# A small HBM-to-HBM copy ahead of the sine load on ScalarE's DMA queue in a rotary embedding kernel

## The chip, the cores and the metric

The kernel runs on one core of a Trainium2 chip. The metric is device time in microseconds (us): the median of the runs shown. Beside the runs there is one profiled execution, whose span goes from its first to its last instruction. The engines of the core are TensorE (PE, with its weight load PEld), VectorE (DVE), ScalarE (ACT), GpSimd (POOL) and SyncE (SP). DMAs are issued from SP (queue q1 in the profile) and from ScalarE (queue q10), and 16 DMA engines carry out both queues' transfers.

## The reference

The input x has the shape 8 x 2048 x 8 x 64 (batch, position, head, feature; float32, 33.55 MB), cos and sin have 2048 x 32 (256 KB each). The 64 features of a head are two halves, and each position turns them by its own angles:

```python
x1, x2 = x[..., :32], x[..., 32:]
out1 = x1 * cos - x2 * sin
out2 = x1 * sin + x2 * cos
return np.concatenate([out1, out2], axis=-1)
```

The output has the shape of x. All of x is read from HBM once and all of the output is written once.

## The kernel before

Positions go to the 128 partitions, 16 of them to each (lines 35 to 38). A batch is so one tile `xt` of 128 x 8192 float32 (4 MB), in which a partition holds 32 KB that lie together in HBM. There are five such buffers (line 45) for eight batches, and the result is written back into the tile in place.

Loads are issued from SP (`load`, lines 64 to 70). Batch 0 comes in three pieces (1, 1 and 2 MB), with the cosine table between the first and the second; the other batches come whole. The sine table is issued on ScalarE's queue, as the first DMA there (line 76). The first five batches are loaded at the start; the load of batch b + 5 is issued when batch b has been stored (lines 192 and 193), because it takes its buffer.

Stores are issued from ScalarE for batches 0 to 6 and from SP for batch 7 (`store`, lines 72 to 74). Batch 0 is stored in two halves, batch 7 in a half and two quarters, the others whole (`shares`, lines 177 to 182).

The work goes piece by piece (`pieces`, lines 170 to 175), mostly 2048 of a batch's 8192 elements per partition. For a piece, GpSimd makes the two products with the sine (line 122; `nsin` is the negated sine), VectorE the product with the cosine (line 129), and then

- kind A: VectorE adds them into `xt` (line 136);
- kind B: TensorE adds them by matmuls with a unit matrix (lines 143 and 144) and ScalarE copies the sum into `xt` (line 145);
- kind C: VectorE makes the product with the sine as well (line 148), TensorE adds, ScalarE copies (lines 160 to 165).

The first piece of batches 1 to 5 is of kind B or C (line 99), all else is of kind A. `keep` holds the instructions of each engine in the order in which they are written. Waits are put in by the framework: each DMA adds to one of a few completion counters, which are given out in turn, and an engine that needs the data, or a later DMA that takes the same counter, waits for it. Between the start and the first piece, ScalarE negates the sine and copies it to PSUM (lines 90 and 91), and VectorE copies the cosine to PSUM (line 93). GpSimd's first product waits for the sine and for the first piece of batch 0.

Of the kernel before, what the change touches and what calls it, by code (L numbers as in the profile page):

```python
# [10 lines left out]
def kernel(  # L11
# [7 lines left out]
    nc = tc.nc  # L19
    keep = tc.keep_in_program_order  # L20
# [51 lines left out]
    def store(b, lo, n):  # L72
        queue = nc.sync if b == last else nc.scalar
        keep(queue.dma_start(out=ov[b, :, lo : lo + n], in_=xts[b][:, lo : lo + n]))  # L74

    keep(nc.scalar.dma_start(out=sin_sb, in_=sin_src))
    for b in range(NBUF):
        load(b)
# [3 lines left out]
        out=eye,  # L82
        in_=eye,
# [140 lines left out]
```

## Time and profile before

| what | before |
|---|---|
| runs, median (lowest to highest) | 163.81 us (163.75 to 164.03), 3 runs |
| profiled execution, its span | 161.8 us (its time outside the span is not recorded) |
| VectorE busy | 140.1 us (87%) |
| GpSimd busy | 138.9 us (86%) |
| TensorE busy | 49.4 us (31%) |
| ScalarE busy | 12.8 us (8%) |
| DMA queues' packet time, share of 16 engines' span | q1 55.5%, q10 42.6% |
| moved by DMA | 67.65 MB, mean 418 GB/s |
| HBM read, written | 34.08 MB, 33.55 MB |
| sine: issued, landed | 0.73 us, 6.46 us |
| first store: issued, landed | 18.36 us, 38.06 us |
| last load landed | 134.32 us |
| last store: issued, landed | 156.0 us, 160.91 us |

The span of the profiled execution is the time from its first to its last instruction; the runs' times also hold what lies around it. Busy shares of engines are averages over the whole span. "Landed" is when the last of the 16 completion counts of a DMA arrived. A DMA packet is what one DMA engine moves in one piece; its record has a start, a duration, a size and a queue, but not the engine.

### The profile page before, as it was taken

The page shows a single profiled execution, that of the slowest core. Times are in us where ns is not written, and L with a number is a line of the kernel's source. Part 1 is how long each engine was busy: PE and PEld are TensorE (multiplying, and loading weights), DVE is VectorE, ACT ScalarE, POOL GpSimd, SP SyncE. Part 2 cuts the span into 40 slices and gives each one's busy share as a digit, 9 for nine tenths or more (in the row PEclk, how much of TensorE's full clock was granted, in tenths as well). Part 3 has the DMA queues.
Part 4 walks back from the last instruction along what each step waited for, and adds up shares of the span by engine and source line. Part 5 has one row for each costly group of instructions (what it writes and reads, how often), then busy time and mean ns, then how long its engine had stood idle before and what let it go on. Part 6 is the DMA issues. An engine that isn't in the chain of part 4 may idle for free.

```text
span 161.8 us, 459 instructions
## 1 busy us (share of the span) xinstructions
PE 49.4 (31%) x80; PEld 18.5 (11%) x80; DVE 140.1 (87%) x66; ACT 12.8 (8%) x14; POOL 138.9 (86%) x70
## 2 busy tenths in 40 slices
PE   0000000597309760978049714972000000000000
PEld 0000000142004220322023301330000000000000
DVE  0297999999999999999999999199989999899950
ACT  3300000002200220021000220022000000000000
POOL 1399997998999999992999959999899997999800
PEclk9999999999975998589957995699655555555555
DMA  5999999999999999899899999999999999999995
GB/s 158 425 454 494 413 308 446 413 470 405 462 405 462 389 502 405 389 510 397 389 510 397 389 512 397 397 502 397 397 488 413 405 478 413 405 478 409 397 419 225
DMA packets 3314, 67.65 MB, mean 418 GB/s; under 512 B 368, under 2 KB 368, under 8 KB 624
## 3 DMA queue, kind: packets, MB, share of 16 engines
q1 hardware_dynamic: 2016, 38.01, 55.5%
q10 hardware_dynamic: 1296, 29.62, 42.6%
q14 instruction: 2, 0.02, 0.0%
HBM read 34.08 MB, written 33.55 MB: 418 GB/s over the span
## 4 chain that ended last, share of the span: by engine, by line
DMA 48%; DVE 37%; POOL 9%; issue 2%; DVEq 0%; SPq 0%; POOLq 0%; ACTq 0%
DMA xt<-in_x_dram 26%; DVE t L129 18%; DMA out_dram<-xt 18%; DVE xt L136 17%; POOL t L122 9%; DMA sin_sb<-in_sin_dram 4%; DVE t L148 1%; DVEq L136 0%; SPq L67 0%; POOLq L122 0%; ACTq L74 0%
## 5 line engine op out<-in xcount | busy, mean ns | idle before, releaser
L122 POOL TENSOR_TENSOR t<-xt,sin_sb 128x1024 f32<-128x1024 f32 (+1 forms) x32 | 70.4, 2199 | 13.5 <-DMA xt<-in_x_dram 8.3
L129 DVE TENSOR_TENSOR t<-xt,cos_ps 128x2048 f32<-128x2048 f32 (+1 forms) x34 | 73.4, 2167 | 0.8
L122 POOL TENSOR_TENSOR t<-xt,nsin 128x1024 f32<-128x1024 f32 (+1 forms) x32 | 70.3, 2196 | 0.0
L136 DVE TENSOR_TENSOR xt<-t,t 128x2048 f32<-128x2048 f32 (+1 forms) x29 | 62.2, 2145 | 8.2 <-POOL t L122 5.5
L143 PE MATMUL o<-t,eye 128*128 128x512 f32 x24 | 17.0, 799 | 23.1 <-DVE t L129 19.6
L160 PE MATMUL o<-t,eye 128*128 128x512 f32 x16 | 12.0, 844 | 37.8 <-DVE t L129 35.6
L144 PE MATMUL o<-t,eye 128*128 128x512 f32 x24 | 14.9, 709 | 0.0
L145 ACT COPY xt<-o 128x1024 f32<-128x1024 f32 x6 | 6.1, 1012 | 45.7 <-PE o L144 45.7
L143 PEld LDWEIGHTS o<-t,eye 128*128 128x128 f32 x24 | 5.5, 256 | 32.5 <-issue 26.5
L160 PEld LDWEIGHTS o<-t,eye 128*128 128x128 f32 x16 | 3.7, 256 | 43.2 <-issue 39.4
L165 ACT COPY xt<-o 128x1024 f32<-128x1024 f32 x4 | 4.0, 1012 | 47.8 <-PE o L161 47.8
L93 DVE COPY cos_ps<-cos_sb 128x512 f32<-128x512 f32 x1 | 0.7, 695 | 6.9 <-DMA cos_sb<-in_cos_dram 6.9
L144 PEld LDWEIGHTS o<-t,eye 128*128 128x128 f32 x24 | 5.6, 234 | 8.2 <-issue 7.6
L161 PE MATMUL o<-t,neye 128*128 128x512 f32 x8 | 6.3, 875 | 0.2
L148 DVE TENSOR_TENSOR t<-xt,sin_ps 128x2048 f32<-128x2048 f32 x2 | 4.6, 2281 | 0.0
L161 PE MATMUL o<-t,eye 128*128 128x512 f32 x8 | 4.1, 592 | 0.0
L161 PEld LDWEIGHTS o<-t,neye 128*128 128x128 f32 x8 | 2.2, 300 | 5.3 <-issue 3.6
L161 PEld LDWEIGHTS o<-t,eye 128*128 128x128 f32 x8 | 1.5, 190 | 1.9 <-issue 1.9
L90 ACT ACT_TABLE_LOAD x1 | 1.3, 1283 | 1.2 <-PEq L208 1.2
L90 ACT ACTIVATE nsin<-sin_sb 128x512 f32<-128x512 f32 x1 | 0.6, 629 | 4.0 <-DMA sin_sb<-in_sin_dram 4.0
L91 ACT COPY sin_ps<-sin_sb 128x512 f32<-128x512 f32 x1 | 0.6, 580 | 0.0
L80 POOL MEMSET eye<- 128x128 f32 x1 | 0.2, 204 | 0.3 <-POOLq L208 0.3
(6 smaller groups left out, 1.0 us busy)
## 6 DMA issues: line engine op xcount, KB each, us to landing
xt<-in_x_dram SPq DMA_DIRECT2D x7, 4096.0 KB, 42.8
out_dram<-xt ACTq DMA_DIRECT2D x6, 4096.0 KB, 27.2
out_dram<-xt ACTq DMA_DIRECT2D x2, 2048.0 KB, 22.3
xt<-in_x_dram SPq DMA_DIRECT2D x2, 1024.0 KB, 6.7
xt<-in_x_dram SPq DMA_DIRECT2D x1, 2048.0 KB, 12.2
out_dram<-xt SPq DMA_DIRECT2D x1, 2048.0 KB, 9.9
out_dram<-xt SPq DMA_DIRECT2D x2, 1024.0 KB, 6.2
sin_sb<-in_sin_dram ACTq DMA_DIRECT2D x1, 256.0 KB, 5.7
```

The costliest lines, as they stand in the source:

```text
L90: keep(nc.scalar.mul(nsin, sin_sb, -1.0))
L93: keep(nc.vector.tensor_copy(cos_ps, cos_sb))
L122: nc.gpsimd.tensor_mul(out=t2u[:, :, u, :].rearrange("p (r h) d -> p r h d", h=H), in0=xu[:, :, 1 - u, :].rearrange("p (r h) d -> p r h d" ...
L129: nc.vector.tensor_mul(out=t1.rearrange("p (r k d) -> p r k d", r=nr, d=Dh), in0=xk, in1=rep(cos_ps[:, r0 : r0 + nr, :], 2 * H),)
L136: keep(nc.vector.tensor_add(out=xt, in0=t1, in1=t2))
L143: nc.tensor.matmul(oc, eye, t1[:, cs], start=True, stop=False)
L144: nc.tensor.matmul(oc, eye, t2[:, cs], start=False, stop=True)
L145: keep(nc.scalar.copy(xt[:, 2 * j * C : 2 * (j + 1) * C], o))
L148: nc.vector.tensor_mul(out=t2.rearrange("p (r k d) -> p r k d", r=nr, d=Dh), in0=xk, in1=rep(sin_ps[:, r0 : r0 + nr, :], 2 * H),)
L160: nc.tensor.matmul(oc, eye, t1u[:, gs, u, :], start=True, stop=False)
L161: nc.tensor.matmul(oc, eye if u else neye, t2u[:, gs, 1 - u, :], start=False, stop=True)
L165: nc.scalar.copy(xu[:, :, u, :], o.rearrange("p (g d) -> p g d", d=Dh))
```

## The change

A copy is issued on ScalarE's queue ahead of the sine. It takes 16 pieces of 512 bytes of batch 0 from x and puts them into the output at the same places. The pieces are the first 512 bytes of each sixteenth of the batch, 256 KB apart. Nothing passes through SBUF. What it writes is x itself, not the rotated values; the stores of batch 0 write the same bytes later, and wait for the copy.

```diff
         queue = nc.sync if b == last else nc.scalar
         keep(queue.dma_start(out=ov[b, :, lo : lo + n], in_=xts[b][:, lo : lo + n]))
 
+    W = 128
+    first = out.rearrange("b (q r) h d -> b q (r h d)", q=16)[0, :, :W]
+    keep(nc.scalar.dma_start(out=first, in_=x.rearrange("b (q r) h d -> b q (r h d)", q=16)[0, :, :W]))
     keep(nc.scalar.dma_start(out=sin_sb, in_=sin_src))
     for b in range(NBUF):
         load(b)
```

The order of the instructions on every engine is otherwise the same. The lines after it move down by three.

## The prediction

> **What bounds the kernel now.** I read the page's slices first, then its DMA queues, then the stretches by time, then the trace's single DMA packets, and the chain of waits last.
>
> The slices of the page give the mean busy share of the 16 DMA engines (tenths) and what they moved, in 40 slices of 4.05 us; below them stands the queues' share of the 16 engines' span (q1 is SP's queue, q10 ScalarE's).
>
> ```profile
> DMA  5999999999999999899899999999999999999995
> GB/s 158 425 454 494 413 308 446 413 470 405 462 405 462 389 502 405 389 510 397 389 510 397 389 512 397 397 502 397 397 488 413 405 478 413 405 478 409 397 419 225
> ...
> q1 hardware_dynamic: 2016, 38.01, 55.5%
> q10 hardware_dynamic: 1296, 29.62, 42.6%
> ```
>
> The two queues fill 98.1% of the engines' span, and only the first and the last slice are not full. The bound is the DMA engines, not VectorE (87%) or GpSimd (86%). The stretches say the same; columns: us, busy us (and count) of PE, PEld, DVE, ACT, POOL, then clock, DMA share and GB/s.
>
> ```profile
> 20.00:22.00 2.00, 0.00 (x0) 0.00 (x0) 1.90 (x2) 0.00 (x0) 2.00 (x2) 1.00 0.79 262
> 22.00:24.00 2.00, 0.00 (x0) 0.00 (x0) 1.97 (x2) 0.00 (x0) 2.00 (x2) 1.00 1.02 344
> ...
> 30.00:60.00 30.00, 20.05 (x32) 7.47 (x32) 29.35 (x13) 3.66 (x4) 29.26 (x14) 0.89 1.00 431
> 60.00:90.00 30.00, 15.85 (x24) 5.86 (x24) 29.38 (x14) 3.42 (x4) 27.00 (x13) 0.77 1.01 437
> 90.00:120.00 30.00, 13.46 (x24) 5.20 (x24) 25.41 (x13) 3.04 (x3) 27.50 (x13) 0.80 1.00 433
> ```
>
> From 30 us on the engines move 431 to 437 GB/s with no gap. There is one dip, slice 5 of the page (counted from 0; 308 GB/s, 20.2 to 24.3 us). Short stretches are rough, because a packet counts where it starts, so I sized the dip by the trace's packets. A load packet of 32 KB takes 1.213 us everywhere else; of those that start from 19.4 to 23.3 us, all 16 engines have some at 1.25 to 2.09 us. What they take beyond 1.213, summed and divided by 16, is 0.39 us per engine for those that start before 22 us and 0.45 us for those after: **0.83 us of every engine lost**, once. Before that there are 0.49 us in the first packets (0.35 to 1.03 us for 8 KB, against 0.309 later) and 0.15 us near 3 us; from 24 us to the end all of it comes to 0.06 us. The dip is where the first store of the run comes in: issued on ScalarE's queue at 18.36 us, its first packet recorded at 22.2 us. All later stores add no such loss, though each batch writes 4 MB of the output not touched before.
>
> The chain of waits names DMA and VectorE by turns:
>
> ```profile
> 62.55 28.82 DMA out_dram<-xt
> ...
> 91.50 42.82 DMA xt<-in_x_dram
> ...
> 134.45 4.62 POOL t L122 x2
> ```
>
> I don't read it as three equal limits. The store issued at 62.55 stands behind the store before it (issued 46.3, landed 72.0), and the load issued at 91.5 behind one that lands at 95.8: both queues always hold work, so an issue some tenths later costs the engines nothing. At the end the last three stores land at 156.05, 158.49 and 160.91 us, 2.43 apart, which is 8 packets of 8 KB at 0.309 (2.47): they too follow the engines' pace.
>
> So time = start of the first packet (1.76 us) + packet time per engine + losses + about 0.9 us after the last packets. An edit counts by what it adds to or takes from the engines.
>
> **The change, part by part.** The sum is made against the profiled span of 161.8 us. The profile gives nothing around it; the runs' median of 163.81 lies 2.0 above, and I leave that as it is.
>
> *One more issue on ScalarE's queue.* The sine's issue row is 0.40 us, the stores' 0.34: sine issue 0.73 -> about 1.1, table load 1.16 -> 1.55. The table load (1.28) ends at 2.8, under ScalarE's wait to 6.48: 0.
>
> *The sine's landing.* At the start each engine takes an 8 KB load packet (0.309) and a 2 KB sine packet (0.084) in turn. With the copy's packet ahead and an issue 0.4 us later, the sine falls one to three turns back, and then has cosine packets (0.084) in its gaps: it lands 0.04 to 0.30 us later than 6.46, I take 0.15. GpSimd waits for it:
>
> ```profile
> POOL t L122 <- DMA xt<-in_x_dram: 8.3, 6, 3.0
> ...
> POOL t L122 <- DMA sin_sb<-in_sin_dram: 5.2, 1, 5.2
> ```
>
> GpSimd and VectorE start that much later, and the first store with them. The cover is the load queue: loads of 4 MB are outstanding until 134.3 us, so engines without a store take loads instead. Cost 0. Later GpSimd waits 8.3 us in all for loads, which swallows the delay. Without that cover it would be 0.15 at the end.
>
> *The copy's own packets.* Sixteen pieces of 512 bytes; I take one per engine. No row shows HBM to HBM. From below: the 4-byte packets, 0.009. From above: a first packet that waits for its read with nothing else under way, 0.72 beyond transfer. The nearest row is a later 2 KB packet (0.084), so 0.03, and 0.009 for its completion: **+0.04**. The Trainium skill, DMA: Bandwidth & Descriptors, section on why a DMA increments its semaphore by 16, has the count of engines as the largest number up to 16 that divides both sides' slowest dimension, so all 16 here; no run yet shows it for such a copy. With the copy on one engine, the other 15 would keep their loss and the time would be 163.85.
>
> *Waits that it adds.* The first store waits for the copy too. In the built program the completion counters shift by one DMA, so SP's load of batch 2 (issued about 3.3 us, no wait before) waits for the copy, and the load of batch 3 for the sine (6.46) instead of the first piece of batch 0 (6.28). Behind them on SP stand the loads of batches 3 and 4 (issued 6.30 and 9.41). The copy should land by 6.5 us like its neighbours; batch 1's load keeps q1 busy until 25 us. Cost 0; cover gone only if the copy took over 20 us.
>
> *The loss at the first store.* The copy is a write to the output by every engine at 2 to 4 us. If the 0.83 us are the price of an engine's first writes to the output, the copy pays that price at the start with 512 bytes instead of 16 KB in flight, partly while engines wait for their first read anyway (0.49 us). Bounds: the whole 0.83 is saved, or nothing, or it is paid twice. For it being the first write: it comes once, at the first store, on all engines. It isn't any waking queue: SP's queue, empty since 134, starts storing near 150 us and nothing stretches. Against it: the load packets that stretch first start before a store packet is recorded. I take the saving, less one more hitch of the size seen near 3 us, when the sine joined the loads: **-0.83 + 0.15 = -0.68**.
>
> Sum: -0.68 + 0.04 = **-0.64 us**: span 161.2, time 163.81 - 0.64 = **163.2**. Nothing else becomes late: the last load lands up to 0.64 earlier; GpSimd had idled 1.14 before its work on it, VectorE 0.64 at 139.09, so both can follow, and the last store's issue moves from 156.0 to 155.4.
>
> **The rivals.**
> 1. *The loss stays* (163.81 + 0.04 = **163.85**). The stretch would be what loads suffer when stores start beside sixteen engines in step: at 20.9 us all are within 0.3 us of each other, after two rounds they are spread over 0.7 us. A copy of 8 KB changes nothing of that. For: two waves, and the stretch before the first store packet; a late sine and a copy that doesn't touch what it should end here too. Against: engines in step from 3 to 20 us lose only 0.02. The Trainium skill, DMA: Bandwidth & Descriptors, section on latency and other measured facts, has HBM latency at 0.2 us on average and 2 us at high load; by that the stretch is load and stays. This trace doesn't bear it out well: from 30 to 120 us the load is higher and nothing stretches.
> 2. *The freeze comes twice* (slower). Writes to HBM freeze the loads whenever they first join them. The copy brings that to the start, and the stores, with far more bytes, still bring theirs at 20 us. Price: the first wave, 0.39, + 0.15 + 0.04 = +0.58: **164.4**; with both waves 164.7. It decides once the start's extra stretch is over 0.33 us and the dip is still there. For: every join of q10 has shown a stretch (0.15 near 3 us). Against: 512 bytes per engine are 1/32 of a store packet.
>
> **How the numbers follow.** About 0.2% (0.33 us) is what a measurement can tell from no change. Forecast 0.48, rival 1 0.33, rival 2 0.19. The forecast's own range is 163.0 (0.83 saved, 0.04 paid) to 163.5 (half saved). For 8 in 10 it has to take in rival 1 and the lower edge of rival 2: 162.9 to 164.2 (163.81 + 0.39). Faster 0.48, same 0.33, slower 0.19.
>
> **What would show it.** Right: slice 5 at 400 GB/s or more, load packets at 1.213 us through 20 to 24 us, the copy landed before 6.5 us, the sine at 6.5 to 6.8, and the last store landing about 0.6 us earlier. Rival 1: the dip unchanged. Rival 2: the dip unchanged and first packets longer than 1.03 us, or the bytes of the first slices well under 158 and 425 GB/s. I'd be wrong throughout if the engines fell idle anywhere, since then issue times would count.

## The result, and the profile after

| what | before | after |
|---|---|---|
| runs | 163.78 us median (163.61 to 164.03, 4 runs) | 168.29 us median (165.17 to 172.79, 4 runs) |
| ratio, 95% interval | | 1.0116 (1.0083 to 1.0150) |
| profiled execution: span | 161.8 us | 163.3 us |
| copy: issued, first packet, landed | | 0.73, 4.67, 5.80 us |
| sine: issued, first packet, landed | 0.73, 2.19, 6.46 us | 1.36, 5.26, 9.53 us |
| first store issued | 18.36 us | 21.49 us |
| last load landed | 134.32 us | 132.18 us |
| VectorE's last addition ends | 156.0 us | 155.2 us |
| last store's 16 completions, first and last | 160.08, 160.91 us | 160.12, 162.51 us |

The ratio takes only runs within 1.5% of the fastest of the same kernel; the changed kernel's runs spread wider than that, which is why its median lies above what the ratio says.

The kernel became slower, by 1.2% by the ratio, outside the range of 162.9 to 164.2. The slices and queues of the changed kernel's page, to be held against those of before:

```profile
DMA  5999999999999989999999999999999999999992
GB/s 191 408 447 481 401 385 389 469 425 401 429 477 425 449 385 473 425 393 481 409 441 449 393 435 425 417 465 401 395 449 433 441 441 409 441 449 397 407 425 102
...
q1 hardware_dynamic: 2016, 38.01, 55.2%
q10 hardware_dynamic: 1328, 29.63, 42.2%
```

The engines are still full from the second slice on, and the dip has only moved, from slice 5 (308) to slices 5 and 6 (385, 389), with the later first store. By the single packets it costs 0.71 us per engine in this profile (0.84 before, both counted from 15 to 30 us). The last slice is the emptier one: 102 GB/s against 225.

The early part of the changed kernel in order of time (start, duration, engine, line, instruction):

```profile
0.73 0.60 ACTq L78 DMA_DIRECT2D out_dram<-in_x_dram  x1
0.73 0.37 SPq L67 DMA_DIRECT2D xt<-in_x_dram  x1
...
1.36 0.60 ACTq L79 DMA_DIRECT2D sin_sb<-in_sin_dram  x1
...
9.67 1.26 POOL L125 TENSOR_TENSOR t<-xt,sin_sb 128x512 f32<-128x512 f32 x1 [8.37 <-DMA sin_sb<-in_sin_dram]
```

GpSimd starts 3.14 us later than before (6.53). Its waits and the DMAs' times to landing show that this is the sine, and that no later load is waited for (before, 8.3 us in 6 waits):

```profile
POOL t L125 <- DMA sin_sb<-in_sin_dram: 8.4, 1, 8.4
```

```profile
sin_sb<-in_sin_dram ACTq DMA_DIRECT2D x1, 256.0 KB, 8.2
out_dram<-in_x_dram ACTq DMA_DIRECT2D x1, 8.0 KB, 5.1
```

Compute made up for the delay, as predicted: its last addition ends 0.8 us earlier than before. The first engine's completion of the last store comes at the same time (160.12 against 160.08). What is late is the last engine, by 2.39 us against 0.83. The lost time is found in the stretches (us, busy us and count of PE, PEld, DVE, ACT, POOL, clock, DMA share, GB/s):

```profile
60.00:90.00 30.00, 16.28 (x27) 5.98 (x26) 29.38 (x14) 3.04 (x3) 28.47 (x13) 0.78 1.01 436
90.00:120.00 30.00, 15.51 (x29) 5.91 (x27) 28.89 (x14) 4.05 (x4) 28.90 (x13) 0.84 1.00 424
```

From 60 to 90 us the engines move as much as before (436 and 437 GB/s), from 90 to 120 less (424 and 433) with the same busy share: packets take longer. Load packets of 32 KB, 1.213 us otherwise, take up to 2.13 us there. What all packets take beyond their usual time comes to 0.61 us per engine from 90 to 125 us (0.53 of it in loads), against 0.05 before. It is not alike on all engines, or the completions of the last store would not lie further apart than before.

### The profile page after: what moved, and what is told of

It reads as the page before. It is cut to its first block, busy times and chain, and to the rows that moved or that the text cites. A ratio compares the mean times of both kernels' runs of the same rounds, so it can differ in the third digit from the quotient of the medians.

```text
span 163.3 us, 460 instructions
## 1 busy us (share of the span) xinstructions
PE 49.4 (30%) x80; PEld 18.6 (11%) x80; DVE 140.1 (86%) x66; ACT 12.8 (8%) x14; POOL 139.0 (85%) x70
## 4 chain that ended last, share of the span: by engine, by line
DVE 75%; POOL 9%; issue 6%; DMA 5%; DVEq 0%; ACTq 0%; POOLq 0%
DVE t L132 39%; DVE xt L139 33%; POOL t L125 9%; DMA sin_sb<-in_sin_dram 5%; DVE t L151 3%; DVEq L139 0%; ACTq L78 0%; POOLq L125 0%
```

## The experiments

Two theories stood at first. L: the copy delays the sine, so all compute and all stores come 3 us later, and that late start does the harm. C: the copy's own writes do it. "Distance" below is the end of batch 4's load minus the end of batch 1's store, each by the median of its 16 completion records in the trace: 4.65 us before (the store ends first), -2.37 after (the load ends first). For batches 5 and 2, and 6 and 3, it is within about 0.1 us of that in both. It belongs to the one run profiled.

### e1: the copy behind the sine

```diff
     keep(nc.scalar.dma_start(out=sin_sb, in_=sin_src))
+    W = 128
+    first = out.rearrange("b (q r) h d -> b q (r h d)", q=16)[0, :, :W]
+    keep(nc.scalar.dma_start(out=first, in_=x.rearrange("b (q r) h d -> b q (r h d)", q=16)[0, :, :W]))
```

> The copy stands behind the sine on ScalarE's queue, so the sine doesn't wait for it. Theory L (the late sine does the harm: the copy's packets come 3.9 us after its issue, the sine behind it lands at 9.5 instead of 6.5 us, and all compute and all stores come 3 us later): sine landed at 6.4 to 6.7 us, time 163.6 to 164.1. Theory C (the copy's own writes to the output do it, whatever the sine does): sine at 6.4 to 6.7 us and still 165 or more. My forecast's saving, if there is one, would show here alone: 163.0 to 163.4, and no stretched load packets at 20 to 24 us.

Measured 163.69 us (163.42 to 166.12, 10 runs), ratio 0.9997 (0.9987 to 1.0007); sine landed at 6.6 us. The dip cost 0.74 us per engine although every engine had written to the output by then. Theory C falls, and so does the saving of my forecast. One of the ten runs, at 166.12, lay apart; of the 31 runs of the kernel before beside it, one did (165.60).

### e2: the sine late without a copy

```diff
-    keep(nc.scalar.dma_start(out=sin_sb, in_=sin_src))
...
+            if b == 0 and lo == UNIT:
+                keep(nc.sync.dma_start(out=sin_sb, in_=sin_src))
```

> No copy. The sine goes to SP's queue behind the second piece of batch 0, so that it lands about as late as with the copy ahead (9.5 to 10.1 us). Theory L: 165 to 166, like the changed kernel, with load packets stretched after 70 us and the last store's 16 completions more than 2 us apart. Theory C: 163.6 to 164.1, since the late start of compute is covered by queued loads, as the prediction had it.

Measured 165.0 us (163.61 to 170.87, 10 runs), ratio 1.0053 (1.0023 to 1.0084). The sine landed at 9.66 us, 0.73 us per engine were lost from 90 to 125 us, and the last store's completions spread over 2.7 us. No copy is needed for the harm, which is half a per cent here; four of the ten runs, from 163.61 to 163.99, show none.

### e3: a load ahead of the sine instead of the copy

```diff
+    W = 128
+    spare = const_pool.tile([16, W], f32, tag="spare")
+    keep(nc.scalar.dma_start(out=spare, in_=x.rearrange("b (q r) h d -> b q (r h d)", q=16)[0, :, :W]))
     keep(nc.scalar.dma_start(out=sin_sb, in_=sin_src))
```

> Instead of the copy, a load of the same 16 pieces of 512 bytes into a spare tile leads ScalarE's queue (the spare tile isn't used). If it is the write to HBM that makes the copy's packets come 3.9 us after the issue, this load's packets come 1.0 to 1.5 us after it, the sine lands at 6.5 to 6.9 us, and by theory L the time is 163.6 to 164.1. If any DMA ahead of the sine delays it, the sine lands at 9 us or later and the time is 165 or more by theory L. By theory C (writes to the output) 163.6 to 164.1 in both cases.

Measured 163.65 us (163.32 to 170.25, 10 runs, two of them above 164), ratio 0.9994 (0.9983 to 1.0006). The load's packets came at 2.37 us, but the sine's only at 5.12, 3.95 after its issue, and it landed at 7.9: neither of the two cases that I had put down. VectorE's first addition starts 1.5 us later than before. The two runs above 164, at 168.73 and 170.25, remain unexplained; the run profiled was not one of them.

### e4: the changed kernel again

No edit.

> The changed kernel as it is, beside the others on one chip. Both theories: 165 to 166, sine landed near 9.5 us, the copy's first packet 3.9 us after its issue.

Measured 168.43 us (163.77 to 170.21, 10 runs), ratio 1.0008 (0.9968 to 1.0047). The medians of the two series agree (168.29 and 168.43), the ratios don't: four runs lie from 163.77 to 164.71, and these alone make the ratio; six lie from 168.43 up. The run profiled took 163.99; in it the sine landed at 9.26 us, and the distance was -2.32. So at nearly the same distance one kernel took 163.99 here and 165.17 in the first series. The dip cost 0.37 us per engine here, not 0.71.

### e5: the first store late, all else on time

```diff
         if b == 0:
-            return [2 * UNIT, 2 * UNIT]
+            return [3 * UNIT, UNIT]
```

> No copy, the sine on time, but batch 0's first store takes three quarters instead of half, so that it is issued near 23.1 us instead of 18.4. If it is the late start of the stores that lets the engines fall in step and lose time (theory L, first form): completions of a DMA within 0.8 us of each other at 38 to 92 us, stretched loads near 74, 94 and 114 us, time 164 to 166. If it is the late compute and not the store (second form): 163.5 to 164.0 and completions 1.5 us apart as before.

Measured 163.66 us (163.49 to 163.93, 10 runs), ratio 1.0003 (0.9994 to 1.0013), though the first store was issued at 23.09 us. This late first store, which is also a larger one, does no harm.

### e6: the changed kernel with an earlier first store

```diff
         if b == 0:
-            return [2 * UNIT, 2 * UNIT]
+            return [UNIT, UNIT, 2 * UNIT]
```

> The changed kernel with batch 0 stored as a quarter, a quarter and a half, so that the first store goes out near 16 us although the sine lands at 9.5. First form of theory L (late stores): 163.5 to 164.1, completions 1.2 us or more apart from 38 us on. Second form (late compute): like the changed kernel, 164 to 166, in step.

Measured 163.55 us (163.41 to 163.73, 10 runs), ratio 0.9995 (0.9986 to 1.0005). Copy and late sine are there, the harm is gone. The sine landed at 8.55 us, and VectorE's first addition starts 2.2 us later than before (3.1 in the changed kernel):

```profile
POOL t L125 <- DMA sin_sb<-in_sin_dram: 7.4, 1, 7.4
```

So a start of compute 2.2 us late does no harm with these stores. With e5 and e6 both simple forms of theory L fall, as far as they can be told apart: both runs also divide the stores of batch 0 otherwise. The completions of one DMA lie 0.7 to 1.9 us apart from 31 us on, partly closer than I had written for that case.

### e7: the copy first, the sine on SP

```diff
-    keep(nc.scalar.dma_start(out=sin_sb, in_=sin_src))
+    keep(nc.sync.dma_start(out=sin_sb, in_=sin_src))
```

> The copy still leads ScalarE's queue, but the sine is issued on SP ahead of the first piece of x. The copy's packets come near 4.7 us all the same; the sine lands by 6.3 us. Theory L: 163.4 to 164.0, like the kernel before. Theory C (the copy itself does harm): 165 or more.

Measured 163.64 us (163.44 to 163.96, 10 runs), ratio 1.0003 (0.9994 to 1.0013). The copy leads its queue and costs nothing. Its first packet came at 2.85 us and not near 4.7:

```profile
sin_sb<-in_sin_dram SPq DMA_DIRECT2D x1, 256.0 KB, 2.8
out_dram<-in_x_dram ACTq DMA_DIRECT2D x1, 8.0 KB, 3.0
```

Here SP's queue opens with the sine, 8 packets of 2 KB for each engine (0.084 us each), where in the changed kernel it opens with x, 8 packets of 8 KB (0.309 each). In both the copy started when those had mostly gone. The row that I had in mind, 3.9 us from issue to first packet for a write to HBM, is no fixed price.

### e8: one more run of the changed kernel

No edit.

> One look at the changed kernel, for one more profile of it. Theory L: sine landed near 9.5 us, compute done by 155.5 us, and what the time has beyond 163.8 lies in load packets over 1.213 us and in the last engine's lag at the end, not in compute.

One run, 170.66 us, span 168.8. The expectation was wrong in one point: compute was late too. Batch 6's load has its first completion at 110.1 us and its last at 119.1; the last engine's lag grew to 9 us, GpSimd waited for it, and the last addition ended at 160.6:

```profile
POOL t L125 <- DMA xt<-in_x_dram: 7.1, 3, 4.1
```

Packets chained by end and start (the records hold no engine, so this is rough) give three or four engines whose store packets took 0.1 to 0.7 us too long, one after the other, from 66 to 118 us, beside engines with hardly any loss.

### e9 to e12: only compute late

The kernel before with GpSimd's first product made again, one to four times; no DMA is touched. e9's list is [2], e10's [2, 2], e11's [2, 2, 1] (the last one half a product), e12's [2, 2, 2, 2]. The delays come out 0.2 to 0.5 us longer than planned.

```diff
+        for m in [2] if (b, lo) == (0, 0) else []:
+            keep(
+                nc.gpsimd.tensor_mul(
+                    out=t2u[:, : m * H, 1, :].rearrange("p (r h) d -> p r h d", h=H),
+                    in0=xu[:, : m * H, 0, :].rearrange("p (r h) d -> p r h d", h=H),
+                    in1=rep(sin_sb[:, :m, :], H),
+                )
+            )
         if kind != "C":
```

> The kernel before, its DMAs untouched, with GpSimd's first product made once more (1.2 us), so that compute and the first store come about 1.2 us late; results are the same. If what matters is how late the store stream stands against the load stream, this lies between the kernel before and the changed one: 163.5 to 164.0. If any delay is covered by queued loads, as predicted: 163.5 to 163.9 here and in the next three.

> The same with two more products, 2.4 us late. Store position decides: 163.6 to 165, the completions of a store and of the load beside it 1 to 2.5 us apart (3.7 to 4.4 before). Covered: 163.5 to 163.9.

> The same with two and a half more products, 3.1 us late, the delay that the changed kernel's sine brings, but with sine, copy and all early DMAs as before. Store position decides: like the changed kernel, 164 to 166 or more, with load packets over 1.213 us after 70 us. If the early DMAs matter (a late sine among the loads of batch 0): 163.5 to 163.9.

> The same with four more products, 4.8 us late. If the harm grows with lateness: 166 or more. If it belongs to one position of the two streams, which this has passed: 163.6 to 164.5, with compute, done near 157, now close behind the DMA engines.

| run | first addition starts later by (planned) | time (runs) | ratio, 95% interval | distance |
|---|---|---|---|---|
| e9 | 1.6 us (1.2) | 168.17 us (165.90 to 170.15, 4) | 1.0196 (1.0126 to 1.0267) | +2.46 us |
| e10 | 2.6 us (2.4) | 167.63 us (164.56 to 170.99, 6) | 1.0095 (1.0053 to 1.0138) | -2.28 us |
| e11 | 3.6 us (3.1) | 164.85 us (164.61 to 166.23, 6) | 1.0084 (1.0055 to 1.0113) | -2.41 us |
| e12 | 5.3 us (4.8) | 164.02 us (163.79 to 164.22, 10) | 1.0022 (1.0012 to 1.0031) | -7.19 us |

A delay of 1.6 us in one engine's work cost 1.4 to 4%, one of 5.3 us cost 0.2%. Harm doesn't grow with lateness. (e12's 0.2% may be compute: its last addition ends at 157.4 us, 1.4 later than before, and the last store's completions lie only 0.1 us apart.) e9 was expected between the two kernels and came out as bad as the changed one. The stretches (columns as above) and the slices of e9's page, which is that of its longest run (170.15 us), show the loss and how it ends:

```profile
60.00:90.00 30.00, 15.91 (x26) 5.70 (x24) 29.38 (x14) 3.04 (x3) 27.67 (x13) 0.77 1.02 424
90.00:120.00 30.00, 13.56 (x25) 5.13 (x24) 26.12 (x12) 4.05 (x4) 23.77 (x11) 0.82 1.00 424
...
DMA  5999999999999998999899999999999999979661
GB/s 156 430 430 479 397 440 417 420 436 436 424 440 452 389 459 366 467 382 459 374 467 405 469 374 452 389 444 420 436 422 428 436 420 405 444 343 436 288 288 55
```

The engines are full, at 424 GB/s instead of 433 to 437, until a few of them lag so far that the others run out of work (7, 9, 6, 6, 1 at the end). In e9 nearly all of the extra packet time up to 125 us is in store packets (0.05 of 1.71 us per engine from 60 us on is in loads). In the changed kernel most of it is in loads.

### e13 and e14: the distance put to the test

New theory P: harm comes at a distance near 2.4 us either way, one load packet and one store packet (2 x 1.213). e13 is e9 with the list [1] (0.65 us planned, 0.9 measured), e14 the changed kernel with the list [2] (1.2 us planned; 0.8 later than the changed kernel's profile, 4.0 later than before).

> The kernel before with compute 0.65 us late (half of GpSimd's first product made once more). Theory P (position): harm comes where the load of a batch and the store three batches back end about 2.4 us apart by the median engine, one load packet and one store packet, either way round; before they end 4.7 us apart. If the store stream's position moves only in whole packets, 0.65 us leaves it at 4.7 and the time at 163.4 to 164.0; if it comes to 2.2 to 2.5 apart, 164.5 or more. Lateness theory (any delay up to 3 us harms): 164.5 or more whatever the distance.

> The changed kernel with its copy, and GpSimd's first product made once more (1.2 us), so that compute is even later, about 4.3 us in all. Theory P: the load now ends before its store by 4.8 us or more instead of 2.4, and the time comes back to 163.5 to 164.2 although more is late. Lateness theory: as the changed kernel or worse, 165 or more.

e13: 168.53 us (163.67 to 168.54, 4 runs), distance +2.47. Three of the four runs lie at 168.52 to 168.54, the other at 163.67, and no ratio is given. Of the 13 runs of the kernel before beside it, 11 lie from 163.47 to 163.74 and two at 174.22 and 292.21, so e13 alone would be thin evidence. My guess that so small a delay leaves the distance alone was wrong; with the distance at 2.5 the harm is there in three runs, as both theories had it. e14: **163.69 us** (163.34 to 164.53, 10 runs), ratio 1.0005 (0.9989 to 1.0021), distance -4.69. The copy is there, the sine is late, compute is later than in the changed kernel, and the time is that of the kernel before. Lateness as the measure falls. But the run profiled (164.33) still lost 0.70 us per engine to long packets from 60 to 125 us, as much as the changed kernel's profile (0.67), so packets stretch at this distance too. The difference lies in how evenly the engines bear it: the last store's completions lie 1.4 us apart, against 2.4.

All kernels by distance. "In pairs" is the same by another measure: the 16 completions of each of the two DMAs are taken in order, the first with the first and so on, and the median of the 16 differences is given. Both belong to the run profiled, whose time stands first; the median of all runs is in brackets.

| distance, us | in pairs, us | kernels, with time in us |
|---|---|---|
| +4.7 | +3.8, +3.9 | before (not recorded; 163.78), e7 163.46 (163.64) |
| +2.7 | +3.4 | e1 163.42 (163.69) |
| +2.5 | +2.4, +2.5 | e9 170.15 (168.17), e13 168.52 (168.53) |
| +0.1 | +1.0 | e3 163.43 (163.65) |
| -2.3 to -2.4 | -2.2 to -2.4 | after 165.17 (168.29), e2 165.29 (165.0), e4 163.99 (168.43), e8 170.66, e10 168.12 (167.63), e11 166.23 (164.85) |
| -4.7 | -3.7 | e14 164.33 (163.69) |
| -5.0 | -5.8 | e5 163.49 (163.66) |
| -7.2 | -7.2 | e12 163.95 (164.02) |
| -9.6 | -9.6 | e6 163.48 (163.55) |

## Why the prediction was wrong

- **The loss at the first store (-0.68), the term that made the forecast.** It failed. In e1, e7 and the changed kernel all engines write to the output long before the first store, and the dip stays: 0.74, 1.03 and 0.71 us per engine. It isn't the price of first writes. The changed kernel has also shown 0.37 and 0.42 (e4, e8), but 0.25 to 0.51 come without a copy as well, in e11, e2 and e12, whose stores also join after 21 us. What sets its size is open. Rival 1 had this right; its second half, that the time then stays, failed.
- **The sine's landing (0.15 us late).** It was 3.07. "One to three turns back" took the copy for a DMA that shares turns with x from the start, as the sine did before. Its issue took 0.60 us instead of 0.40, its first packet came at 4.67, when the 8 packets of x's first piece had left each engine, and the sine stood behind it. The Trainium skill, DMA: Bandwidth & Descriptors, section on queues, rings and completion order, has an engine drain a whole packet of one queue, typically 9 to 17 descriptors, before it turns to the next. If each 8 KB record is one descriptor, the copy's wait for 8 of them would be near that, but the sine before took turns record by record from 2.19 us on; no run here settles which holds.
- **"Cost 0: the load queue covers it."** This is the step that cost the sign. The cover itself held: engines stayed full, compute caught up and ended 0.8 us earlier than before. What I left out is that loads ahead of their usual place change which load packets run beside which store packets for the next 100 us, and that this can have a price: 0.67 us per engine in long packets from 60 to 125 us (0.05 before), borne so unevenly that the last engine ended 1.6 us later than before. Nothing in the trace of before shows it, since there the distance stays at 4.2 to 4.7; but the sum took "full engines" for "constant packet times". e9 shows the price with no DMA edited, only compute's start put off.
- **The copy's own packets (+0.04).** Right: 16 packets of 0.027 us, and e1 and e7 cost nothing. Its 16 completions arrive one by one from 5.2 to 5.8 us, so that the count of engines that the Trainium skill gives (DMA: Bandwidth & Descriptors, section on why a DMA increments its semaphore by 16) agrees with the trace.
- **Waits added.** Right: SP's load of batch 2 waited 2.4 us for the copy and that of batch 3 3.4 us for the sine, and the queue never ran dry.
- **Rival 2 (164.4).** Its sign was right and its mechanism not: the first packets lost no more than before (0.41 against 0.49 us up to 2.5 us). The loss came after 90 us, where no rival looked. (Its 164.7 for both waves leaves out the 0.15 that its 164.4 counts; with it the sum is 164.8.)

What is shown: in the changed kernel the late sine turns the sign. With the copy but the sine on time, the time is that of the kernel before (e1, e7); a late sine without a copy harms (e2), and so does late compute with no DMA touched (e9, e10, e11). How late compute starts does not set the harm: 1.6 us harms (e9), 4.0 doesn't (e14), and 5.3 costs 0.2% (e12). The granted clock doesn't either: 83 of the 86 runs of the kernel before, taken beside the experiments, took 163.4 to 164.1 us at 0.761 to 0.772, and the changed kernel's runs from 168.43 us up show 0.761 to 0.768.

What is argued: that the distance decides. Profiled runs at 2.2 to 2.5 us either way, by both measures, took 163.99 to 170.66 us, all others 163.42 to 164.33. In long packets from 60 to 125 us the first lose 0.60 to 1.99 us per engine, the others 0.05 to 0.11, but e14 0.70. No run sets the distance alone, and it doesn't fix the time: at -2.3 the changed kernel took 163.99 (e4) and 170.66 (e8).

**Open** is why 2.4 us, and what decides between a short and a long run there. Engines in step can't be it alone. The number of engines at a store packet at once, from 45 to 85 us, has a standard deviation of 6.4 in the changed kernel, but also 6.1 in e3 and e12, whose profiled runs are short; it is 5.0 in e9 and 3.5 before. Whether it matters which addresses in HBM the two streams touch at the same time is untested: no run varied addresses.

## What to carry to other kernels

Where DMA engines are full, don't count a shifted transfer as free: two streams' packets can take longer for much of the run after a small shift of one of them, and a few engines can fall behind. Try several small shifts of the start (a repeated instruction is enough) before blaming or crediting an edit. A tiny DMA ahead of one that others wait for can cost that one its turn beside the other queue, here 3.07 us.

## What the runs showed of the hardware

- The time from a DMA's issue to its first packet was no fixed price beside a busy queue: for the copy it was 3.9 us beside 8 KB packets (the changed kernel) and 2.1 beside 2 KB packets (e7), for the sine issued level with x 1.5 us (before), for a load of 512-byte pieces 1.6 and for the sine behind it 3.95 (e3).
- With full engines, a load that ended 2.3 to 2.5 us before or after the store three batches back went with profiled runs of 163.99 to 170.66 us, single engines up to 9 us behind; other distances went with 163.42 to 164.33.
- The stretched 32 KB packets from 60 to 125 us were nearly all stores at +2.5 (e9, e13) and mostly loads at -2.3 to -2.4 in four profiles of six (after, e2, e4, e11).
- With half a product more on GpSimd, which made the first addition 0.9 us later, three of four runs took 168.5 us, beside 163.6 for the kernel before (e13).
